# Reading the second layer's modulation rows in the two mixers instead of the first MLP's second product

## The chip, the cores and the metric

The kernel runs on one core of a Trainium2 chip, in one launch. The metric is device time in microseconds (us) of that launch, lower being better. The engines that matter here are TensorE (PE, matrix products, with its weight loads shown apart as PEld), VectorE (DVE), ScalarE (ACT), GpSimd (POOL, which here mostly issues transfers) and SyncE (SP, which issues most transfers, in order). Each engine works off its own list of instructions in order; semaphores tie the lists together.

## The reference, cut to what matters

The program is a trunk of two layers over a sequence of 1024 positions and width 1024. A conditioning vector c modulates every sub-layer:

```python
cond = jax.nn.silu(c)
for i in range(DEPTH):
    mod = cond @ ada_w[i] + ada_b[i]
    sh1, sc1, g1, sh2, sc2, g2 = jnp.split(mod[:, None, :], N_MOD, axis=-1)
    h = _modulate(_rmsnorm(x, norm_mix_g[i]), sh1, sc1)
    y = _s5_mixer(h, ...) if i % N_MIXERS == 0 else _ssd_mixer(h, ...)
    x = x + g1 * y
    h = _modulate(_rmsnorm(x, norm_mlp_g[i]), sh2, sc2)
    x = x + g2 * _sq_relu_mlp(h, mlp_w1[i], mlp_w2[i])
return _rmsnorm(x, final_norm_g)
```

The product `cond @ ada_w[i]` gives 6 x 1024 numbers for each layer. The kernel cuts each layer's into 48 rows: one row is a block of 128 output columns, whose 128 x 1024 weights (512 KB) are read and multiplied with the conditioning vector. Eight rows make one of the six vectors (shift, scale and gate of the mixer, then of the MLP). For the second layer the first two vectors (16 rows) are needed when the first MLP ends, since its output is normalised and modulated there for the second mixer; the third when the second mixer's output is added; the fourth to sixth in the second MLP.

## The kernel before, in words

Activations lie with the 1024 channels over eight blocks of 128 partitions and the sequence along the free dimension, in two halves of 512. Every matrix product is made of three passes: weights and activations are each split into a high part and a remainder, and `mm3` (lines 117 to 119) multiplies high by high, high by low and low by high. So each 512 KB weight tile is loaded by SP into one of four buffers of the pool `raw` (line 95), ScalarE writes its high part `whi` (line 84), VectorE its low part `wlo` (line 85), and only then is the load buffer free. The pair `whi`, `wlo` lies in a ring of further buffers, and is free again when TensorE has used it for both halves of the sequence.

The stages follow each other: the first mixer (S5) with its gated projection `glu` at 285 to 453 us, the first MLP's up product (`Up`) and second product (`mlp_down`) from 775 to 1098 us, the second mixer (`ssd_proj` and `ssd_group`) to about 1660 us, its output product, and the second MLP with the same two products (the second one from 2188 to 2498 us).

The gated projection runs over four passes (`mg` 0 to 3). A pass has two output blocks m, each with a value weight and a gate weight, so four weights of 512 KB, over both halves. The weights of the next pass are asked for at the end of a pass, and behind them the caller asks for modulation rows.

The second product of an MLP runs over seven sub-products of eight steps. A step loads and combines a weight tile, loads activations that were stored to memory, splits both on ScalarE and VectorE and makes 24 matmuls. The second mixer makes, for each of four groups of heads, six blocks of a convolution and four blocks of the gate z, each a weight tile over both halves; the chunks of the group before are worked off between these.

A modulation row is `mod_dot` (lines 329 to 334): SP loads the 512 KB, VectorE makes the dot product with an accumulator in one instruction (line 334), and after eight rows the bias is added (line 317). Where no pool of its own is named (`K.adap`), the row is loaded into the pool `raw`, so that it takes a turn among the weights' four load buffers; in the first MLP's second product it has two buffers of its own.

The code gives the order in which work is asked for. The order on each engine is set from it by a list scheduler when the program is built, and is fixed from then on.

## Time and profile before

| what | value |
|---|---|
| median of 3 runs | 2514.36 us (2514.31 to 2516.89) |
| span of the profiled execution | 2516.1 us |
| mean granted TensorE clock | 0.989 |
| TensorE, VectorE, ScalarE busy | 97%, 76%, 46% |
| DMA queue of SP and ScalarE, share of 16 engines | 47.8% |
| rows (line 334) | 88, 1220 ns each |

The profile is of one execution. Its times are us from the start of the span. Busy time by engine says how full an engine is; the chain of waits says which work ended last; the order of time and the busy time by stretches say what a single stage waits for. "PEclk" or "granted clock" is the share of full speed that TensorE was allowed. A row of the order of time has the start, the duration, the engine, the line, the operation and the tiles (written <- read), and in brackets how long the engine had been idle and what ended that. "SPq" rows are transfers being issued. The 88 dot products of line 334 are 40 of the first layer's 48 rows (the mixer's shift is made on TensorE) and the 48 of the second layer, of which the profile shows the latter from 796 to 1040 us.

### The profile page before, as it was taken

The page shows a single profiled execution, that of the slowest core. Times are in us where ns is not written, and L with a number is a line of the kernel's source. Part 1 is how long each engine was busy: PE and PEld are TensorE (multiplying, and loading weights), DVE is VectorE, ACT ScalarE, POOL GpSimd, SP SyncE. Part 2 cuts the span into 40 slices and gives each one's busy share as a digit, 9 for nine tenths or more (in the row PEclk, how much of TensorE's full clock was granted, in tenths as well). Part 3 has the DMA queues.
Part 4 walks back from the last instruction along what each step waited for, and adds up shares of the span by engine and source line. Part 5 has one row for each costly group of instructions (what it writes and reads, how often), then busy time and mean ns, then how long its engine had stood idle before and what let it go on. Part 6 is the DMA issues. An engine that isn't in the chain of part 4 may idle for free.

```text
span 2516.1 us, 32759 instructions
## 1 busy us (share of the span) xinstructions
PE 2445.6 (97%) x11624; PEld 1961.2 (78%) x11624; DVE 1913.1 (76%) x3265; ACT 1167.4 (46%) x1975; POOL 214.4 (9%) x400
## 2 busy tenths in 40 slices
PE   7999899999999999999999999999999999999997
PEld 3788788877777778877887878877888777788886
DVE  8798754978887898968585867789687777787664
ACT  4577412744444334534464645534246444444342
POOL 0010000122221000100000000000011222210000
PEclk8999999999999999999999999999999999999998
DMA  6576773467769999823554554574246666794752
GB/s 244 149 174 165 237 251 97 148 205 258 263 226 318 322 307 320 276 85 109 162 160 153 159 168 145 180 249 141 80 137 210 217 223 222 256 318 150 252 191 84
DMA packets 284643, 503.80 MB, mean 200 GB/s; under 512 B 22080, under 2 KB 162368, under 8 KB 284480
## 3 DMA queue, kind: packets, MB, share of 16 engines
q1 hardware_dynamic: 242496, 386.34, 47.8%
q0 software_dynamic: 32384, 106.98, 12.5%
q10 hardware_dynamic: 9600, 8.39, 1.0%
q8 instruction: 91, 1.49, 0.2%
q14 instruction: 72, 0.59, 0.1%
HBM read 364.27 MB, written 133.17 MB: 198 GB/s over the span
## 4 chain that ended last, share of the span: by engine, by line
PE 80%; DVE 7%; DMA 5%; ACT 3%; issue 2%; DVEq 0%; SPq 0%; ACTq 0%
PE pd L117 11%; PE pd L118 11%; PE pd L119 11%; PE py L117 4%; PE py L119 4%; PE py L118 4%; PE px L117 4%; PE px L119 3%; PE px L118 3%; PE pv L117 3%; PE pv L118 3%; PE pv L119 3%; PE pm L119 2%; PE pm L117 2%; PE pm L118 2%
## 5 line engine op out<-in xcount | busy, mean ns | idle before, releaser
L84 ACT CAST whi<-raw 128x1024 fp32r<-128x1024 f32 x241 | 251.0, 1047 | 360.5 <-PE pd L118 145.4
L85 DVE TENSOR_TENSOR wlo<-raw,whi 128x1024 fp32r<-128x1024 f32 x241 | 293.0, 1217 | 107.8 <-ACT whi L84 104.2
L334 DVE SCALAR_TENSOR_TENSOR ada<-ada,cond 128x1024 f32<-128x1024 f32 x88 | 107.0, 1220 | 57.6 <-DMA ada<-in_ada 57.3
L499 ACT ACTIVATE s<-s 128x512 f32<-128x512 f32 x84 | 53.0, 631 | 156.1 <-DVE s L497 153.6
L391 POOL DMA_DIRECT2D hscr<-x x32 | 17.4, 543 | 955.4 <-DVE x L758 752.5
L1257 DVE SCALAR_TENSOR_TENSOR cacc<-cr,conv,cacc 128x1024 f32<-128x1024 f32 x72 | 91.7, 1277 | 1.0 <-ACT cacc L1238 0.6
L1310 ACT ACTIVATE L<-csb,cs 128x128 f32<-128x128 f32 x224 | 69.9, 390 | 39.8 <-DMA csb<-csr 39.8
L506 POOL DMA_DIRECT2D b<-s x96 | 52.0, 542 | 319.9 <-ACT s L500 278.5
L497 DVE TENSOR_TENSOR s<-s,px 128x512 f32<-128x512 f32 x60 | 41.0, 683 | 34.4 <-PE px L119 34.4
L497 DVE TENSOR_TENSOR s<-s,pv 128x512 f32<-128x512 f32 x36 | 24.7, 686 | 55.1 <-PE pv L119 55.1
L506 POOL DMA_DIRECT2D b<-tt x96 | 52.0, 542 | 44.8 <-DVE tt L511 27.9
L500 ACT ACTIVATE s<-s 128x512 f32<-128x512 f32 x84 | 53.2, 633 | 2.7
L1261 ACT ACTIVATE cth<-cacc 128x512 f32<-128x512 f32 x48 | 27.7, 624 | 42.3 <-DVE cacc L1257 40.4
L673 DVE SCALAR_TENSOR_TENSOR x<-py,mod,x 128x512 f32<-128x512 f32 x40 | 27.6, 743 | 24.4 <-PE py L119 24.4
L209 ACT ACTIVATE sq<-x 128x512 f32<-128x512 f32 x28 | 16.7, 625 | 54.1 <-DVE x L673 49.1
L1330 DVE SCALAR_TENSOR_TENSOR y<-xs,cst,pm 128x128 f32<-128x128 f32 x128 | 38.2, 340 | 4.7 <-PE pm L1327 4.7
L117 PE MATMUL pd<-h00h,whi 128*128 128x512 f32 (+1 forms) x97 | 39.9, 413 | 1.8 <-ACT h00h L238 1.8
L1237 ACT COPY cr<-pd 128x512 f32<-128x512 f32 x48 | 27.8, 579 | 28.8 <-PE pd L119 28.8
L1128 ACT ACTIVATE gt<-pd,bgh 128x512 f32<-128x512 f32 x16 | 11.0, 685 | 63.9 <-PE pd L119 63.9
L117 PE MATMUL pd<-h01h,whi 128*128 128x512 f32 x97 | 39.5, 407 | 0.5 <-DVE h61h L758 0.5
L119 PE MATMUL pd<-h10h,wlo 128*128 128x512 f32 (+1 forms) x97 | 39.3, 405 | 0.0
L118 PE MATMUL pd<-h30l,whi 128*128 128x512 f32 (+1 forms) x97 | 38.9, 401 | 0.0
(1006 smaller groups left out, 8165.1 us busy)
## 6 DMA issues: line engine op xcount, KB each, us to landing
raw<-in_w SPq DMA_DIRECT2D x204, 512.0 KB, 4.7
br<-b SPq DMA_DIRECT2D x112, 512.0 KB, 5.4
ada<-in_ada SPq DMA_DIRECT2D x96, 512.0 KB, 5.3
b<-s POOLq DMA_DIRECT2D x96, 256.0 KB, 2.9
b<-tt POOLq DMA_DIRECT2D x96, 256.0 KB, 3.8
csb<-csr SPq DMA_DIRECT2D x32, 512.0 KB, 4.6
raw<-in_w_xbc SPq DMA_DIRECT2D x24, 512.0 KB, 4.3
xscr<-cacc SPq DMA_DIRECT2D x24, 512.0 KB, 2.7
```

The source lines that it names most:

```text
L84: K.nc.scalar.copy(hi, src)
L85: K.nc.vector.tensor_tensor(lo, src, hi.bitcast(F32), op=ALU.subtract)
L117: K.nc.tensor.matmul(ps, wh, xh, start=start and i == 0, stop=False, skip_group_check=more)
L118: K.nc.tensor.matmul(ps, wh, xl, start=False, stop=False, skip_group_check=more)
L119: K.nc.tensor.matmul(ps, wl, xh, start=False, stop=stop and i == n - 1, skip_group_check=more)
L334: K.nc.vector.scalar_tensor_tensor(r, r, 1.0, K.cond, op0=ALU.mult, op1=ALU.mult, accum_out=acc)
L497: nc.vector.tensor_tensor(t, t, p, op=ALU.add)
L499: nc.scalar.activation(t, t, AF.Relu)
L500: nc.scalar.activation(t, t, AF.Square)
L506: self.K.nc.gpsimd.dma_start(self.bscr[DOWN.index(nm)][m // 2][m % 2], t)
L1257: V.scalar_tensor_tensor(acc, cr[:, t:t + L], K.cw[:, i, t:t + 1], acc, op0=ALU.mult, op1=ALU.add)
L1310: nc.scalar.activation(Lm[:, r, :], cb[:, r, :], AF.Relu, bias=S.cs[:, c0 + r:c0 + r + 1], scale=-1.0)
```

## The change

The 48 rows of the second layer no longer belong to `mlp_down`; its parameter `extra` and the two calls of it are gone, as is the row pool's use there. The first 16 (shift and scale of the second mixer) are appended to the rows of the gated projection, which asks for up to 11 after each pass instead of up to 6: 11, 11 and 10 now, where it was 6, 6 and 4. The other 32 are asked for in the second mixer, one before each half of a z block (the condition `left < KT` holds for the eight yields of these halves in each group). In both places they use the pool `raw`. The conditioning vector's tile, 4 KB of each partition, stays allocated until the end of the second mixer.

```diff
-def mlp_down(K, pool, x, bscr, w2, gate, xscr, mid, extra):
+def mlp_down(K, pool, x, bscr, w2, gate, xscr, mid):
...
-        if q == 0:
-            extra()
-        if q not in (4, 5):
-            extra()
...
-        K.adap = K.br if cond else None
-        mlp_down(
-            K, K.br, x, K.bscr[i], io.w2[i], gate, K.hscr[i], lambda *a: mid(x, *a), lambda: next(mods, None)
-        )
-        drain(mods)
-        K.adap = None
+        mlp_down(K, K.br, x, K.bscr[i], io.w2[i], gate, K.hscr[i], lambda *a: mid(x, *a))
...
-    mod0 = mods(K, io.ada, 0, (3, 4))
+    def rows(*of):
+        for i, js in of:
+            yield from mods(K, io.ada, i, js)
+
+    mod0 = rows((0, (3, 4)), (1, (0, 1)))
...
     for _ in glu(K, x, io.x, g, io.s5_w_glu, us, begun, io.ada, mid):
-        for _ in range(6):
+        for _ in range(11):
             next(mod0, None)
...
-    mod1 = mods(K, io.ada, 1, (0, 1, 2, 3, 4, 5))
...
-    cond.release()
+    mod1 = mods(K, io.ada, 1, (2, 3, 4, 5))
...
-    pr = ssd_proj(K, cp, h, 0)
+
+    def project_in(g):
+        for left in ssd_proj(K, cp, h, g):
+            if left is not None and left < KT:
+                next(mod1, None)
+            yield left
+
+    pr = project_in(0)
...
-        pr = ssd_proj(K, cp, h_mix, gr)
+        pr = project_in(gr)
...
+    drain(mod1)
+    cond.release()
```

The order on the engines moves in three places. The first is SP's list of transfers in the gated projection, before the change. `raw<-in_s_w_glu` are the four weights of the fourth pass, `ada` are rows, `x` are tiles of the residual, and `raw<-in_w` the first weights of the MLP that follows.

```order
L333 DMA ada<-in_ada 128x1024
L268 DMA x_2791<-in_x 128x512
L268 DMA x_2792<-in_x 128x512
L268 DMA x_2789<-in_x 128x512
L268 DMA x_2790<-in_x 128x512
L333 DMA ada<-in_ada 128x1024 x6
L95 DMA raw<-in_s_w_glu 128x1024 x4
L333 DMA ada<-in_ada 128x1024 x6
L95 DMA raw<-in_w 128x1024 x21
```

The same piece with the change:

```order
L333 DMA ada<-in_ada 128x1024 x2
L268 DMA x_2791<-in_x 128x512
L268 DMA x_2792<-in_x 128x512
L333 DMA ada<-in_ada 128x1024 x3
L268 DMA x_2789<-in_x 128x512
L333 DMA ada<-in_ada 128x1024 x5
L268 DMA x_2790<-in_x 128x512
L333 DMA ada<-in_ada 128x1024 x2
L95 DMA raw<-in_s_w_glu 128x1024 x4
L333 DMA ada<-in_ada 128x1024 x12
L95 DMA raw<-in_w 128x1024 x21
```

Behind the fourth pass's weights stand twelve rows instead of six (ten rows and the two of the residual's gate that the fourth pass uses), and the batch before them is thirteen instead of eight.

The second place is VectorE's list in the same stage, at the end of the third pass. Before:

```order
L334 SCALAR_TENSOR_TENSOR ada,mac_3594<-ada,cond 128x1024
L1131 TENSOR_TENSOR x_2796<-x_2796,gv 128x512
L373 SCALAR_TENSOR_TENSOR mod<-mac_3594,cst 128x1
L374 TENSOR_SCALAR g1h<-mod 128x1
L1129 TENSOR_SCALAR gt<-gt,g1h 128x512
L1130 SCALAR_TENSOR_TENSOR gv<-pd,cst,gt 128x512
L1131 TENSOR_TENSOR x_2793<-x_2793,gv 128x512
L85 TENSOR_TENSOR wlo<-raw,whi 128x1024 x2
```

With the change (line numbers above 584 are four lower in the new kernel; `gt`, `gv` and `x` are the gating of a finished half):

```order
L1126 SCALAR_TENSOR_TENSOR gv<-pd,cst,gt 128x512
L334 SCALAR_TENSOR_TENSOR ada,macc<-ada,cond 128x1024
L1127 TENSOR_TENSOR x_2796<-x_2796,gv 128x512
L334 SCALAR_TENSOR_TENSOR ada,macc<-ada,cond 128x1024 x4
L1125 TENSOR_SCALAR gt<-gt,g1h 128x512
L1126 SCALAR_TENSOR_TENSOR gv<-pd,cst,gt 128x512
L334 SCALAR_TENSOR_TENSOR ada,macc<-ada,cond 128x1024
L1127 TENSOR_TENSOR x_2793<-x_2793,gv 128x512
L317 SCALAR_TENSOR_TENSOR mod<-macc,cst 128x8
L323 SCALAR_TENSOR_TENSOR G<-mod,cst 128x8
L334 SCALAR_TENSOR_TENSOR ada,mac_3639<-ada,cond 128x1024
L85 TENSOR_TENSOR wlo<-raw,whi 128x1024
```

The last row of each piece is the low part of the fourth pass's first weight (with the second weight's behind it before the change). Between the weight converted ahead of it and this one stood three rows; now nine do, seven of them in this piece.

The third place is VectorE's list in the second mixer, in one of the chunks of a group. `cr` and `cacc` belong to the convolution, `yz`, `L`, `ysq`, `ssq` and `st` to the chunk.

```order
L1278 TENSOR_TENSOR yz<-y,zl 128x512
L1308 TENSOR_SCALAR L<-csb,ncs 128x128
L1227 MEMSET cr 128x3
L334 SCALAR_TENSOR_TENSOR ada,macc<-ada,cond 128x1024
L1278 TENSOR_TENSOR ysq<-ysq 128x256
L1278 TENSOR_TENSOR ysq<-ysq 128x128
L1253 SCALAR_TENSOR_TENSOR cacc<-cr,conv,cacc 128x1024
L1348 COPY ssq<-pm 128x1
L1278 TENSOR_TENSOR st<-st,pm 128x512
```

The row stands among the chunk's own steps, where there was none; of a group's eight rows four stand so, one for each of four chunks, and the other four among the z blocks of the group before.

More of the change, by code (lines that the diff above doesn't have):

```diff
@@ L1467, in left, with mlp @@
         return tc.alloc_tile_pool(name=name, bufs=n, reuse_waits="tile")
-    def mlp(i, x, xa, up, pan, gate, mid, cond=None, mods=(), gates=()):
-        mods, gates = iter(mods), iter(gates)
+    def mlp(i, x, xa, up, pan, gate, mid, gates=()):
+        gates = iter(gates)
         K.wz = right("wz" + str(i), 2)
@@ L1642, in mid @@
         return norm_steps(K, x, f, each, bank, order)
-    mlp(0, x, xa, up, up.pan, modv(K, 0, 5), mid, True, mod1, gate0)
-    cond.release()
+    mlp(0, x, xa, up, up.pan, modv(K, 0, 5), mid, gate0)
+    mod1 = mods(K, io.ada, 1, (2, 3, 4, 5))
     K.wx = left("wx1", 2)
@@ L1678, in trunk @@
     x, x1 = h_new(), h_new()
-    h_mix = h
     up, mid = entry(1, x1, K.G[:, 24:32], modv(K, 1, 3))
```

## The prediction

> **What bounds the kernel now.** I read the page first, then the busy time by stretches, then the order of time around the places that the change touches.
>
> ```profile
> span 2516.1 us, 32759 instructions
> PE 2445.6 (97%) x11624; PEld 1961.2 (78%) x11624; DVE 1913.1 (76%) x3265; ACT 1167.4 (46%) x1975; POOL 214.4 (9%) x400
> PE 80%; DVE 7%; DMA 5%; ACT 3%; issue 2%; DVEq 0%; SPq 0%; ACTq 0%
> ```
>
> TensorE is busy 97% of the span and makes 80% of the chain of waits. So moving VectorE or DMA work is worth something only where TensorE stands still for it, or runs at a lower clock afterwards. The change leaves TensorE's own work alone. The question is which TensorE pauses go and which come.
>
> The kernel holds a control experiment: the second product of the MLP runs twice, in the first layer with the 48 rows and in the second without any. The columns are length, then busy time of PE, PEld, DVE, ACT, POOL, then granted clock, DMA share and GB/s.
>
> ```profile
> 775.00:1098.00 323.00, 315.51 (x1361) 256.81 (x1360) 272.92 (x427) 134.40 (x228) 19.05 (x35) 0.98 0.86 294
> 2188.00:2498.00 310.00, 309.99 (x1360) 254.19 (x1359) 211.23 (x311) 129.49 (x217) 10.92 (x20) 1.00 0.63 212
> ```
>
> The same work (1360 and 1359 weight loads recorded), 13.0 us apart. The difference sits in the second and third of the seven sub-products; the fourth, and the same two of the second layer, follow:
>
> ```profile
> 820.00:870.50 50.50, 47.25 (x195) 38.11 (x194) 43.57 (x76) 14.77 (x31) 3.28 (x6) 0.93 0.93 312
> 870.50:919.00 48.50, 45.74 (x193) 36.91 (x192) 47.93 (x81) 21.17 (x37) 0.00 (x0) 0.96 0.95 315
> 919.00:963.00 44.00, 44.00 (x193) 36.01 (x193) 43.09 (x66) 16.62 (x24) 0.00 (x0) 1.00 0.94 323
> 2232.20:2276.30 44.10, 44.10 (x194) 36.12 (x193) 40.98 (x68) 19.25 (x37) 2.74 (x5) 1.00 0.81 266
> 2276.30:2320.10 43.80, 43.80 (x194) 36.05 (x193) 29.04 (x43) 17.92 (x28) 0.00 (x0) 1.00 0.39 129
> ```
>
> 50.5 + 48.5 − 44.1 − 43.8 = 11.1 us. Of this 3.25 + 2.76 = 6.0 us are two pauses of TensorE, (1 − 0.93) × 50.5 + (1 − 0.96) × 48.5 = 5.5 us a lower clock. The pauses in the order of time, with the matmul before and two after the first:
>
> ```profile
> 849.21 0.39 PE L118 MATMUL pm<-h21l,whi 128*128 128x512 f32 x1
> 852.84 0.79 PE L119 MATMUL pm<-h21h,wlo 128*128 128x512 f32 x1 [3.25 <-DVE wlo L85]
> 853.86 0.63 PE L118 MATMUL pn<-h21l,whi 128*128 128x512 f32 x1
> 886.41 0.80 PE L119 MATMUL py<-h41h,wlo 128*128 128x512 f32 x1 [2.76 <-DVE wlo L85]
> ```
>
> Both end when VectorE delivers a weight's low part: the rows stand ahead of it on a VectorE that is 86% and 99% busy. The matmuls behind the pause take 0.63 instead of 0.39 us.
>
> **What is removed.** 48 rows (a 512 KB load and an L334 dot product) leave the stretch 775 to 1098. Its second copy says what is left: **−11.1 us** for the two sub-products. The other 1.9 us of the 13.0 lie at the stretch's entry and at its closing normalisation, which the rows need not cause. Bounds: −6 (one of the two pauses has another cause) to −13. I take −11.
>
> [...]
>
> **What is added in the gated projection.** 16 rows go to the stretch 285 to 453, where TensorE has hardly a pause so far and VectorE idles 41%:
>
> ```profile
> 285.00:453.40 168.40, 167.69 (x745) 137.90 (x744) 99.19 (x169) 42.99 (x56) 7.61 (x14) 1.00 0.55 181
> L334 DVE SCALAR_TENSOR_TENSOR ada<-ada,cond x22: 1214/1225/1227, 306.9 to 387.3; 128x1024 f32<-128x1024 f32 x22
>   DMA ada<-in_ada: 27.7, 15
> DMA to landing us min/median/max: 3.4/4.6/6.5
> ```
>
> VectorE time alone would be 16 × 1.3 = 21 us into 69 us of idle time: free. But the rows share four buffers and one in-order queue with the weights, and in that order nine of them now stand ahead of the first weight of the fourth pass, where three stood. I call its four weights, in the order in which VectorE converts them, w3, w4, w1, w2 (TensorE needs w1 first). Before:
>
> ```profile
> 362.08 1.22 DVE L85 TENSOR_TENSOR wlo<-raw,whi 128x1024 fp32r<-128x1024 f32 x1 [2.33 <-ACT whi L84]
> 366.84 1.23 DVE L334 SCALAR_TENSOR_TENSOR ada<-ada,cond 128x1024 f32<-128x1024 f32 x1 [1.62 <-DMA ada<-in_ada]
> 378.40 1.22 DVE L85 TENSOR_TENSOR wlo<-raw,whi 128x1024 fp32r<-128x1024 f32 x1 [0.76 <-ACT whi L84]
> 381.54 1.23 DVE L334 SCALAR_TENSOR_TENSOR ada<-ada,cond 128x1024 f32<-128x1024 f32 x1 [1.91 <-DMA ada<-in_ada]
> 384.40 1.23 DVE L334 SCALAR_TENSOR_TENSOR ada<-ada,cond 128x1024 f32<-128x1024 f32 x1 [1.22 <-DMA ada<-in_ada]
> 387.28 1.23 DVE L334 SCALAR_TENSOR_TENSOR ada<-ada,cond 128x1024 f32<-128x1024 f32 x1 [0.41 <-DMA ada<-in_ada]
> 400.17 1.23 DVE L85 TENSOR_TENSOR wlo<-raw,whi 128x1024 fp32r<-128x1024 f32 x1 [3.54 <-ACT whi L84]
> ...
> 352.79 7.32 SPq L95 DMA_DIRECT2D raw<-in_s_w_glu  x4
> 363.34 19.80 SPq L333 DMA_DIRECT2D ada<-in_ada  x6
> ...
> 404.95 0.39 PE L119 MATMUL pd<-h00h,wlo 128*128 128x512 f32 x1
> ```
>
> w1 is done at 401.4 and needed at 404.95: 3.6 us to spare. It cannot be done sooner, since its buffer is freed by the third pass at 400. Its raw copy and w2's hold two of the four load buffers, so the rows in between go through the other two, one every 2.9 us (381.54, 384.40, 387.28), and through one buffer while w4 waits too: 3.5 us from the issue at 363.34 to 366.84, plus 1.3.
>
> Step one, when the fourth pass's weights arrive. Ten more rows (five in each of the first two batches) go ahead of their loads. The present pace, and the idle time that can take some of it:
>
> ```profile
> 332.52 1.23 DVE L334 SCALAR_TENSOR_TENSOR ada<-ada,cond 128x1024 f32<-128x1024 f32 x1 [6.44 <-DMA ada<-in_ada]
> 338.20 1.23 DVE L334 SCALAR_TENSOR_TENSOR ada<-ada,cond 128x1024 f32<-128x1024 f32 x1 [2.46 <-DMA ada<-in_ada]
> 344.39 1.22 DVE L334 SCALAR_TENSOR_TENSOR ada<-ada,cond 128x1024 f32<-128x1024 f32 x1 [3.41 <-DMA ada<-in_ada]
> 355.01 1.23 DVE L334 SCALAR_TENSOR_TENSOR ada<-ada,cond 128x1024 f32<-128x1024 f32 x1
> ```
>
> Six rows start from 344.39 to 355.01, 2.1 us apart, so ten are 21 us, less 6.4 + 2.5 + 3.4 = 12.3 us of waiting that is filled at best: at least 9 us late. I take 12: w3 is converted at 374 instead of 362.
>
> Step two: first row 374 + 1.2 + 4.8 = 380, second 385, w4 at 386, then nine rows at 2.9 us with the first of them already on its way: 386 + 4 + 8 × 2.9 = 413. w1 follows, done at about 414.5. TensorE needs it at 405: a **pause of about 9 us**, and by the pairs above (6.0 us of pauses, 5.5 of clock) some 2 us at a lower clock behind it; the clock loss of one pause was 3.5 and 1.9 us. Together **+11 us**. Upper end 13 (9.5 + 3.5). Lower end: nothing late in step one gives w4 at 379.6 as now, 381 + 8 × 2.9 + 1.2 = 405.4, a pause of 0.5 us. The other weights have room: w2 is behind one more row and needed 5.4 us after w1.
>
> Behind the waiting rows on VectorE stand also the gating of the two halves finished at 395 and 406. Their PSUM banks are wanted again two halves later, over 20 us, so they cost nothing. The first MLP's weight loads, queued behind the twelve rows on SP, come some 25 us later than at 385.66 and are first used at 453.
>
> **What is added in the second mixer.** 32 rows, eight in each of four groups of heads. In each of the last three groups about four fall into the light stretch and four, one per chunk, into this one (first two rows; the third is the light one):
>
> ```profile
> 1260.00:1300.00 40.00, 39.93 (x211) 31.77 (x210) 35.10 (x63) 26.39 (x51) 0.00 (x0) 1.00 0.54 166
> 1300.00:1340.00 40.00, 40.00 (x230) 32.43 (x229) 36.21 (x66) 23.65 (x53) 0.00 (x0) 1.00 0.59 192
> 1340.00:1380.00 40.00, 39.22 (x191) 31.70 (x190) 18.05 (x41) 15.93 (x33) 0.00 (x0) 1.00 0.44 133
> ```
>
> 80 − 35.1 − 36.2 = 8.7 us of idle VectorE takes four rows of 1.3 us, and each row's load is issued a chunk (some 16 us) before VectorE comes to it, so landing (6.5 us at most above) is covered. The stretch 919 to 963 is the nearest row: VectorE 98% busy, eight rows in it, TensorE 44.00 of 44.00. Cover gone, all twelve such rows cost 16 us. But TensorE's order moves too. A group's last two chunks have 3 and 15 matmuls fewer to cover the way to their final reductions, 18 × 0.23 = 4.1 us (0.23 is 44.00 us over 193 in the stretch 919 to 963). VectorE is lighter there, since the convolutions are through. Bounds: −1 (the 0.8 us pause in the third row goes) to 3 × 4.1 = 12; I take **+2**, three times the 0.7 us of the last chunk, which has a pause already.
>
> **Sum.** −11 + 11 + 2 = +2 us. The profiled execution's span, 2516.1, would become 2518.1; it is one execution, and the median of the three runs is 2514.36, 1.7 less. On that basis: **2516 us**.
>
> **Rivals.**
>
> *The projection holds (faster).* If the loads of the fourth pass arrive in time, its pause is 0.5 us: −11 + 0.5 + 1 = −9.5, 2505 us (1 for a calmer mixer). For it: VectorE idles 41% there and no TensorE pause names it now. Against it: w1 has only 3.6 us to spare behind nine rows on two buffers, and even six us less delay leaves a pause of 3 us.
>
> *VectorE becomes the bound in the chunks (slower).* Place: 1260 to 1340 and the two stretches like it. A row may cost 8.7 / 4 = 2.2 us before the chunk chain falls behind TensorE; it does if a row waits over 0.9 us for its load. The fifteen rows in the projection that waited did so for 27.7 / 15 = 1.85 us; then 1.3 + 1.85 − 2.2 = 0.95 us × 12 = 11 us, and the total is −11 + 11 + 11, 2525 us. The matmuls that cover less (12 us) would end at the same time. For it: 90% busy, in order. Against: the chunk of lead, and the 98% stretch without a pause.
>
> *The first MLP gains little.* If only the 6.0 us of pauses return and the lower clock has another cause, the total is −6 + 11 + 2 = +7, 2521 us; the same if late loads make the pauses (DMA 0.93 busy and more there) and half stays. Against both: the second layer's copy, at clock 1.00 with DMA 0.81 and 0.39. [...] That the rows are not moved at all is excluded by the order of instructions.
>
> **Chances and range.** Forecast 0.48, with its own range of 2511 to 2521; the projection holds 0.26; chunks bound 0.18; little gained 0.08. A difference under 0.2% (5 us) cannot be told from none here. Faster is the first rival and hardly any of the forecast: 0.27. Slower is the other two and a part of the forecast above 2519.4: 0.31. Same: 0.42. The range takes in the first and most of the second rival: 2504 to 2526.
>
> **What would show it.** In the first MLP's second product the two pauses gone, clock 1.00, its length near 311 us. In the gated projection one TensorE pause at about 405 that a weight's low part ends, of 4 to 12 us, with clock below 1.00 behind it. In the mixer no pause over 1.5 us. The forecast is wrong if the projection keeps its length, if the first MLP keeps its pauses, or if the mixer's pauses add up to more than 6 us.

## The result, and the profile after

| | before | with the change |
|---|---|---|
| median | 2514.65 us (2514.31 to 2516.89, 4 runs) | 2539.24 us (2532.74 to 2541.56, 4 runs) |
| ratio | 1 | 1.0094, 95% interval 1.008 to 1.0109 |
| span of the profiled execution | 2516.1 us | 2539.8 us |
| mean granted TensorE clock | 0.989 | 0.987 |

The change makes the kernel 24.6 us slower. The forecast was 2516 us with a range of 2504 to 2526, so it was wrong. One execution among those reported below, 6159 us with the other quotas in the gated projection where the other three took 2524 to 2526 us, is left out of its ratio. The head of the profile's page with the change:

```profile
span 2539.8 us, 32827 instructions
PE 2454.3 (97%) x11624; PEld 1964.6 (77%) x11624; DVE 1914.1 (75%) x3265; ACT 1169.9 (46%) x1975; POOL 214.5 (8%) x400
```

TensorE has the same 11624 matmuls and VectorE the same 3265 instructions in 1914.1 us (1913.1 before). Nothing was added to the work. TensorE's busy time rose by 8.7 us, for the most part matmuls at a lower clock (it was busy for 48.3 us at half clock, 35.8 before), and its idle time by 15.0 us (2539.8 − 2454.3 against 2516.1 − 2445.6). To see where, the matmuls of both traces are counted in order and the same one is compared at each boundary between stages. How much longer each stage became (profiled executions, us):

| stage, by the times of before | change |
|---|---|
| up to 301 (ahead of the rows that moved) | −1.1 |
| gated projection, 301 to 480 | +11.6 |
| first MLP's up product, 480 to 787 | +2.9 |
| first MLP's second product, 787 to 1099 | −12.1 |
| second mixer and its output product, 1099 to 1875 | +24.1 |
| second MLP's up product, 1875 to 2196 | −0.9 |
| the rest | −0.8 |

**The first MLP's second product** gave back what was expected. By stretches, the whole and then two that together hold the second and third sub-products (833.6 to 921.5 us), which had the two pauses (length, busy PE, PEld, DVE, ACT, POOL, granted clock, DMA share, GB/s):

```profile
788.50:1099.00 310.50, 309.81 (x1360) 254.04 (x1359) 219.68 (x322) 137.63 (x228) 19.05 (x35) 1.00 0.66 225
...
833.50:880.00 46.50, 46.50 (x205) 38.09 (x204) 43.49 (x72) 20.91 (x40) 2.74 (x5) 1.00 0.74 251
880.00:922.00 42.00, 42.00 (x186) 34.56 (x185) 26.89 (x40) 16.78 (x26) 0.00 (x0) 1.00 0.41 138
```

310.5 us instead of 323.0, TensorE busy all the time in both stretches, clock 1.00.

**The gated projection** shows the predicted pause. VectorE's list in order of time, the fourth pass's weights being the three L85 rows (w3, w4, w1), with the rows between the first and the last of the nine left out; then TensorE's first matmul that needs w1, and SP's issue of the twelve rows:

```profile
374.39 1.23 DVE L85 TENSOR_TENSOR wlo<-raw,whi 128x1024 fp32r<-128x1024 f32 x1 [1.81 <-ACT whi L84]
379.40 1.23 DVE L334 SCALAR_TENSOR_TENSOR ada<-ada,cond 128x1024 f32<-128x1024 f32 x1 [3.78 <-DMA ada<-in_ada]
384.19 1.23 DVE L334 SCALAR_TENSOR_TENSOR ada<-ada,cond 128x1024 f32<-128x1024 f32 x1 [1.56 <-DMA ada<-in_ada]
385.57 1.22 DVE L85 TENSOR_TENSOR wlo<-raw,whi 128x1024 fp32r<-128x1024 f32 x1
388.99 1.23 DVE L334 SCALAR_TENSOR_TENSOR ada<-ada,cond 128x1024 f32<-128x1024 f32 x1 [2.19 <-DMA ada<-in_ada]
...
410.72 1.23 DVE L334 SCALAR_TENSOR_TENSOR ada<-ada,cond 128x1024 f32<-128x1024 f32 x1 [0.50 <-DMA ada<-in_ada]
411.87 1.22 DVE L85 TENSOR_TENSOR wlo<-raw,whi 128x1024 fp32r<-128x1024 f32 x1
```

```profile
413.14 0.80 PE L119 MATMUL pd<-h00h,wlo 128*128 128x512 f32 x1 [9.15 <-DVE wlo L85]
...
375.65 34.04 SPq L333 DMA_DIRECT2D ada<-in_ada  x12
```

Nine rows from 388.99 to 410.72 are 2.7 us apart, w1 is done at 413.1 and TensorE has waited 9.15 us.

**The second mixer** is where the 24 us came from. The sums over the stretch from the same first to the same last matmul (1098 to 1675 us before, 1099 to 1700 us now), before and after:

```profile
sum 577.00, PE 573.11 PEld 458.74 DVE 430.82 ACT 300.00 POOL 1.14; mean PE 143.28 PEld 114.69 DVE 107.70 ACT 75.00 POOL 0.28
```

```profile
sum 601.00, PE 583.37 PEld 463.70 DVE 466.30 ACT 298.49 POOL 1.14; mean PE 145.84 PEld 115.92 DVE 116.57 ACT 74.62 POOL 0.28
```

601 − 577 = 24 us, of which TensorE's idle time rose from 3.9 to 17.6 us (13.7) and its busy time by 10.3 us, most of it lower clock behind the pauses (TensorE was busy for 15.4 us in four stretches at 0.50; before the change the clock was 1.00). VectorE took 35.5 us more, about what 32 rows of 1.2 us come to, but it still idles 135 of 601 us: it is not full. Its idle time in front of the rows there, and the time from a row's issue to its landing:

```profile
  DMA ada<-in_ada: 30.9, 11
...
DMA to landing us min/median/max: 3.4/4.2/7.7
```

VectorE stood still 30.9 us, in front of 11 of the 32 rows. The worst place is the first chunk of each group. `ysq` is the sum of squares that VectorE makes in two steps and TensorE finishes at line 1347. VectorE, then TensorE, then SP's issues in the order of time:

```profile
1232.96 0.43 DVE L1278 TENSOR_TENSOR ysq<-ysq 128x256 f32<-128x256 f32 x1 [0.70 <-ACT ysq L1343]
1236.87 1.23 DVE L334 SCALAR_TENSOR_TENSOR ada<-ada,cond 128x1024 f32<-128x1024 f32 x1 [3.48 <-DMA ada<-in_ada]
1238.02 0.08 DVE L334 DVE_READ_ACCUMULATOR ada<-ada,cond 128x1 f32 x1
1238.02 0.29 DVE L1278 TENSOR_TENSOR ysq<-ysq 128x128 f32<-128x128 f32 x1
```

```profile
1238.45 0.56 PE L1347 MATMUL pm<-ones,ysq 128*128 128x1 f32 x2 [3.50 <-DVE ysq L1278]
...
1386.83 0.35 PE L1347 MATMUL pm<-ones,ysq 128*128 128x1 f32 x2 [4.34 <-DVE ysq L1278]
...
1537.57 0.56 PE L1347 MATMUL pm<-ones,ysq 128*128 128x1 f32 x2 [3.80 <-DVE ysq L1278]
```

```profile
1228.61 1.22 DVE L85 TENSOR_TENSOR wlo<-raw,whi 128x1024 fp32r<-128x1024 f32 x1
...
1228.12 0.92 SPq L1338 DMA_DIRECT2D zl<-zscr  x2
1229.10 0.49 SPq L95 DMA_DIRECT2D raw<-in_w_z  x1
1229.86 0.35 SPq L333 DMA_DIRECT2D ada<-in_ada  x1
```

A row stands between the two steps of the reduction. It waits 3.48 us for its own load, TensorE's matmul behind it 3.50 us. The load went out at 1229.86 us, when a weight's conversion (1228.61 + 1.22) had given its buffer back, right behind a weight's and two `zl` loads, and its data were there at 1236.84 us. That is 7.0 us from issue to landing; the rows in front of the other two pauses took 7.7 and 7.3 us, and these three are the slowest of the 32 (median 4.2). So two things make such a row late: when its load goes out, and how long it takes there.

### The profile page after: what moved, and what is told of

Same layout as the page of the kernel before. It is cut to its first block, busy times and chain, and to the rows that moved or that the text cites. A ratio compares the mean times of both kernels' runs of the same rounds, so it can differ in the third digit from the quotient of the medians.

```text
span 2539.8 us, 32827 instructions
## 1 busy us (share of the span) xinstructions
PE 2454.3 (97%) x11624; PEld 1964.6 (77%) x11624; DVE 1914.1 (75%) x3265; ACT 1169.9 (46%) x1975; POOL 214.5 (8%) x400
## 4 chain that ended last, share of the span: by engine, by line
issue 63%; PE 22%; POOL 6%; DVE 3%; DMA 3%; ACT 1%; POOLq 0%; DVEq 0%; SPq 0%; ACTq 0%
POOL b L506 3%; PE py L117 2%; PE py L119 2%; PE py L118 2%; PE pm L117 1%; PE pm L118 1%; PE pm L119 1%; PE pd L118 1%; PE pd L117 1%; PE pd L119 1%; PE pm L1081 1%; PE px L117 1%; PE px L119 1%; PE px L118 1%; POOL hscr L391 1%
## 5 line engine op out<-in xcount | busy, mean ns | idle before, releaser
L85 DVE TENSOR_TENSOR wlo<-raw,whi 128x1024 fp32r<-128x1024 f32 x241 | 293.4, 1218 | 99.7 <-ACT whi L84 94.3
L119 PE MATMUL pd<-h00h,wlo 128*128 128x512 f32 (+1 forms) x97 | 38.9, 401 | 9.2 <-DVE wlo L85 9.2
L628 DVE TENSOR_TENSOR raw<-raw 128x1024 f32<-128x1024 f32 x16 | 19.6, 1225 | 30.8 <-DMA raw<-in_w 27.5
L118 PE MATMUL pd<-h11l,whi 128*128 128x512 f32 x97 | 39.4, 406 | 0.0
L1323 PEld LDWEIGHTS pm<-L,xdt 128*64 128x64 f32 x512 | 27.3, 136 | 15.5 <-DVE L L1278 8.4
```

The lines of the kernel that those rows point to most:

```text
L85: K.nc.vector.tensor_tensor(lo, src, hi.bitcast(F32), op=ALU.subtract)
L118: K.nc.tensor.matmul(ps, wh, xl, start=False, stop=False, skip_group_check=more)
L119: K.nc.tensor.matmul(ps, wl, xh, start=False, stop=stop and i == n - 1, skip_group_check=more)
```

## The experiments

Fifteen kernels were run, each against the kernel before on the same chip. In the diffs "-" is the changed kernel, and "..." stands for lines left out. "Stage" times are changes against the kernel before by the same matmul, as in the table above, from one profiled execution each. Where a stage is the same as with the change, they say how far to trust them: the projection shows +10.4 to +12.9 us in seven such runs, the mixer +19.2 to +26.1 in three.

### Where the rows stand in the mixer, and whether they are loaded

The first run moves the rows in the mixer, the second takes their loads away.

```diff
-            if left is not None and left < KT:
+            if left is not None and 5 <= left <= 12:
```

> The changed kernel, but in the second mixer the eight rows of a group are asked for earlier: before the last five halves of the convolution blocks and the first three halves of the z blocks, so that no row stands between the two halves of the first chunk's reduction. The work is the same. Late loads (a row that waits for its own load holds up the reduction behind it): the three pauses of 3.5 to 4.3 us at 1238, 1387 and 1538 us go, with the half clock behind them; 16 to 22 us of the mixer's 24 us come back, about 2520 us. VectorE's work (32 dot products too many for the mixer, wherever they stand): within 3 us of 2539. TensorE's own order (fewer matmuls to cover the last chunks): within 5 us of 2539.

Measured: 2529.44 us (ratio 1.0067, 1.0045 to 1.0089), 15.1 us over the kernel before on its chip, where the change was 24.6 us over. In the profiled execution (span 2525.5 us) the mixer and its output product cost +6.6 us instead of +24.1. The three pauses of the first chunks are gone; what stays in the chunks are two elsewhere, of the same kind:

```profile
1343.65 1.23 DVE L334 SCALAR_TENSOR_TENSOR ada<-ada,cond 128x1024 f32<-128x1024 f32 x1 [1.52 <-DMA ada<-in_ada]
1344.80 0.08 DVE L334 DVE_READ_ACCUMULATOR ada<-ada,cond 128x1 f32 x1
1344.80 0.75 DVE L1278 TENSOR_TENSOR ysq<-ysq 128x256 f32<-128x256 f32 x2
```

```profile
1345.69 0.35 PE L1347 MATMUL pm<-ones,ysq 128*128 128x1 f32 x2 [1.60 <-DVE ysq L1278]
...
1488.37 0.35 PE L1347 MATMUL pm<-ones,ysq 128*128 128x1 f32 x2 [2.79 <-DVE ysq L1278]
```

The same 32 dot products at other places cost a quarter in the mixer: VectorE's work as such is not the price. The total came 9 us above the 2520 expected; its four runs lie 13.6 us apart (2522.34 to 2535.91), so the sum is less sure than the stage.

```diff
-    K.nc.sync.dma_start(r, w)
-    K.nc.vector.scalar_tensor_tensor(r, r, 1.0, K.cond, ..., accum_out=acc)
+    if not K.noload:
+        K.nc.sync.dma_start(r, w)
+    K.nc.vector.scalar_tensor_tensor(
+        r, K.cond if K.noload else r, 0.0 if K.noload else 1.0, K.cond, ..., accum_out=acc)
```

> The changed kernel, but the 32 rows of the second mixer are not loaded: the dot product runs on the conditioning vector, times zero, with the same size and the same buffer, so the second layer's gate of the mixer and its MLP's shift, scale and gate are left out of the computation (only their biases remain). Late loads: the mixer is within 4 us of its time before the change, about 2519 us in all, although a row still stands between the halves of a reduction. VectorE's work: the mixer stays above +18 us, over 2533 us. TensorE's own order: the pauses stay, over 2530 us.

Measured: 2518.56 us (ratio 1.0018, 1.0008 to 1.0028); mixer +3.2 us. One row now stands ahead of the same reduction and one between its two steps, and they hold it up only by their own length:

```profile
1229.81 1.22 DVE L335 SCALAR_TENSOR_TENSOR ada<-cond 128x1024 f32<-128x1024 f32 x1
...
1230.96 0.42 DVE L1279 TENSOR_TENSOR ysq<-ysq 128x256 f32<-128x256 f32 x1
1231.29 1.22 DVE L335 SCALAR_TENSOR_TENSOR ada<-cond 128x1024 f32<-128x1024 f32 x1
1232.44 0.08 DVE L335 DVE_READ_ACCUMULATOR ada<-cond 128x1 f32 x1
1232.44 0.28 DVE L1279 TENSOR_TENSOR ysq<-ysq 128x128 f32<-128x128 f32 x1
```

So the loads make about 21 of the 24 us; 32 dot products without them cost 3. Both runs also moved some of TensorE's and VectorE's instructions in the mixer, so the order was not held fixed; that it is the loads is also read directly from the rows above, where TensorE's pauses of 3.50, 4.34 and 3.80 us follow VectorE's waits of 3.48, 4.22 and 3.84 us for a row's data.

### The gated projection

Loads taken away from the rows asked for after its passes (same edit as above), and the same rows with other quotas:

> The changed kernel, but the rows of the gated projection that are asked for after its passes are not loaded: their dot products run on the conditioning vector, times zero (the first MLP's shift and scale and the second mixer's shift and scale are left out of the computation). Late loads behind four shared buffers: no pause of 9 us at 404 to 413 us, that stage is within 2 us of its time before the change, 2526 to 2529 us in all. VectorE's own work ahead of the fourth pass's weight: a pause of at least 5 us stays there, over 2533 us.

```diff
+    q = [16, 14, 2, 0]
...
-        for _ in range(11):
+        for _ in range(q.pop(0)):
             next(mod0, None)
```

> The changed kernel with the same 40 rows in the gated projection, but 16, 14 and 2 of them asked for after its first three passes instead of 11, 11 and 10, so that four rows instead of nine stand on VectorE ahead of the fourth pass's first weight. If these nine make the pause, it is under 1 us there and 2525 to 2529 us in all. If the sum of loads through four buffers makes it, a pause of over 5 us stays there or moves to the pass before, 2533 us or more.

Measured: 2524.61 us (1.0034 to 1.0064), a little under what was expected, and 2525.07 us (1.0028 to 1.0059); in both the pause is gone and the stage's cost is 0.0 us instead of +11.6. With the other quotas all 40 rows are still loaded, and the fourth pass's first weight is converted when its buffer is free:

```profile
397.16 1.22 DVE L334 SCALAR_TENSOR_TENSOR ada<-ada,cond 128x1024 f32<-128x1024 f32 x1
400.67 1.22 DVE L85 TENSOR_TENSOR wlo<-raw,whi 128x1024 fp32r<-128x1024 f32 x1
```

Four rows stand ahead of it now. So it is the nine rows ahead of that weight, with their loads, and neither their number in the stage nor the bytes.

### Each part undone alone

Rows of the undone part go to the first MLP's second product, with two buffers of their own as before, but asked for later and one at a time: for the projection's 16 rows steps of `q in (2, 3)`, as in the diff, for the mixer's 32 rows `q in (2, 3, 5, 6)`.

```diff
+        if q in (2, 3):
+            extra()
...
-    mod0 = rows((0, (3, 4)), (1, (0, 1)))
+    mod0 = rows((0, (3, 4)))
...
-        for _ in range(11):
+        for _ in range(6):
```

> The changed kernel with only the gated projection's part undone: its quotas are 6 again, and the 16 rows of the second mixer's shift and scale are read in the first MLP's second product, one per step of the third and fourth sub-products, from two buffers of their own. The 32 rows stay in the second mixer. If the parts add up (+11.6 us there), 2524 to 2529 us. If the rows cost again where they go, 2532 us or more.

> The changed kernel with only the mixer's part undone: the 32 rows are read in the first MLP's second product, one per step of the third, fourth, sixth and seventh sub-products and four behind them, from two buffers of their own. The 16 rows stay in the gated projection. If the parts add up (+24 us in the mixer), 2514 to 2519 us. If the 32 rows bring back a pause in that product, 2521 to 2526 us.

Measured: 2526.11 us (1.0037 to 1.0065) with the projection undone, 2518.67 us (1.0011 to 1.0034) with the mixer undone. The parts add up. By stages: projection 0.0 and mixer +25.4 in the first, projection +11.0 and mixer −1.3 in the second. The second product kept −12.1 and −10.8 us, with 16 and 32 rows in it. VectorE does not take these rows in the sub-product where they are asked for, but mostly earlier: in the first to fifth sub-product 1, 7, 8, 0 and 0 of them start with the projection undone, and 1, 7, 12, 8 and 4 with the mixer undone. Before the change it was 7, 15, 9, 9 and 2, and six in the sixth. So rows are free in the second and third sub-products too, seven in one and twelve in the other, and the two pauses of before go with 22 rows in the first two. The one pause left over 1 us (1.02 us, mixer undone) is in the fifth.

### Spreading the rows

Three versions take the rows to other places, to test that a row is free wherever nothing waits behind it, and to find a kernel faster than both. The first has eight rows in the first MLP's up product (behind the eight of its own gate, which move from its fifth step to its first), 32 at `q in (2, 3, 4, 5)` of the second product and eight in the second MLP's up product.

> None of the 48 rows in the gated projection or the second mixer: eight in the first MLP's up product, 32 in its second product but only one per step of sub-products two to five (third to sixth) with two buffers of their own, and eight in the second MLP's up product. If the loss in the second product before the change came from the rows' density in its first sub-products (two, then one per step, where VectorE and the transfers are fullest), the 11 us come back and nothing is paid elsewhere: 2502 to 2507 us. If any row in that product costs, 2510 to 2516 us.

Measured: 2515.00 us (0.9993 to 1.0012), no gain. That lies in the second range that was expected, but only a part of the price is in the second product (−8.3 us instead of −12.1, a pause in the fifth sub-product); the larger part, +10.9 us, is in the first MLP's up product.

```profile
537.81 0.50 PE L117 MATMUL px<-h01h,whi 128*128 128x512 f32 x1 [3.31 <-DVE s L490]
...
981.64 0.50 PE L118 MATMUL py<-h61l,whi 128*128 128x512 f32 x1 [1.85 <-DVE h61l L85]
```

Eight rows more, with the gate's eight moved forward, cost nearly as much in the up product as 48 did where they had been.

> The 48 rows once more without the places that paid: none in the gated projection, none in the first MLP's up product, none in the fifth sub-product of its second product. 24 rows in that product (one per step of the third, fourth and sixth sub-products, own buffers), eight at the first group's convolution in the second mixer, before any chunk runs, eight in the second mixer's output product, eight in the second MLP's up product. If rows cost only where VectorE is full or where they wait for a shared buffer in front of a reduction or weight, all of these are free, and the 11 us of the first MLP's second product stay: 2503 to 2507 us. If any row costs about 0.25 us wherever it stands (the 11 us over 48), 2512 to 2517 us.

Measured: 2508.07 us (0.9965 to 0.9984): 6 us faster than before the change, a little outside the expected range. Two stages showed a price. In the fifth sub-product TensorE pauses for 2.33 us at 973.18. The rows are not what stands there, as was expected of the next run: the last of this product's 24 starts on VectorE at 931.28 us, in the fourth. VectorE waits for a weight's load instead, and why that load is late is not shown:

```profile
968.66 1.23 DVE L628 TENSOR_TENSOR raw<-raw 128x1024 f32<-128x1024 f32 x1 [3.77 <-DMA raw<-in_w]
```

And the second MLP's up product cost +3.1 us; with the same eight rows at the same place it showed −0.6 in the run before, so no price of the place is shown.

```diff
+        if q in (2, 3, 6):
+            extra()
+        if q == 6:
+            extra()
...
+            if left is not None and 5 <= left <= 12:   # first group of heads only: eight rows
...
-    drain(outs)
+    for at in outs:                    # the second mixer's output product: 16 rows
+        next(mod2, None)
+        if at[0] == 2:
+            next(mod2, None)
```

> The spread of 48 rows without the two places that still showed a cost: no row in the sixth sub-product of the first MLP's second product (its rows were pulled ahead into the fifth, where a pause of 2.3 us stood) and none in the second MLP's up product (some 3 us there). Instead: 16 rows in the third and fourth sub-products, one per step, eight in the seventh, two per step; eight at the first group's convolution; 16 in the second mixer's output product. If the remaining costs were of these places, 2502 to 2506 us. If rows cost as much in the output product, 2507 to 2511 us as the spread before.

Measured: 2505.23 us (2502.97 to 2511.44, 12 runs), ratio 0.9972 (0.9961 to 0.9982): 7.3 us faster than the kernel before, the best of all, and within what was expected. Its stages: projection 0.0, second product −12.1, mixer and output +0.1.

```profile
span 2501.8 us, 32801 instructions
PE 2437.7 (97%) x11624; PEld 1957.2 (78%) x11624; DVE 1912.1 (76%) x3265; ACT 1170.8 (47%) x1975; POOL 213.7 (9%) x400
```

Its second, third and fourth sub-products, in which 8, 12 and 3 rows start (the rows asked for in the seventh are taken as early as these):

```profile
819.00:863.00 44.00, 44.00 (x193) 36.06 (x192) 43.48 (x73) 19.17 (x38) 2.73 (x5) 1.00 0.97 341
863.00:907.00 44.00, 44.00 (x195) 36.20 (x194) 39.00 (x66) 18.10 (x29) 0.00 (x0) 1.00 0.71 240
907.00:951.00 44.00, 44.00 (x194) 36.03 (x193) 35.90 (x49) 16.77 (x24) 0.00 (x0) 1.00 0.83 279
```

### Why the mixer's rows get their data late

Four ways to get a row's data sooner: a fifth shared buffer (with its control), an earlier request, another queue, and buffers of their own.

```diff
-    K.raw = perm("raw", bufs=4)
+    K.raw = perm("raw", bufs=5)
...
-    return K.tmp.tile([P, 512], F32, tag="t", bufs=6, name=name)
+    return K.tmp.tile([P, 512], F32, tag="t", bufs=4, name=name)
```

> The changed kernel with five load buffers instead of four in the pool that rows and weights share; to make room, the pool of temporaries of 512 columns has four buffers instead of six. If a free load buffer is what late loads wait for, the pause in the gated projection shrinks from 9 us to under 4 (rows go through three buffers, some 2.0 us apart instead of 2.7) and the mixer's loss from 24 us to under 14: 2516 to 2528 us. If loads are late because they are asked for late, or because they land slowly, 2533 us or more.

> The control for the one before: the changed kernel with only the temporaries' pool cut from six to four buffers, four load buffers as they were. If these temporaries matter nowhere, within 3 us of 2539; if they do, slower, and the run with five load buffers is read against this one.

Measured: 2625.54 us with five buffers and 2637.88 us for the control, so the expected totals were off by 100 us for a reason outside the question: four temporaries cost +46.0 and +52.1 us in the two up products. By stages against the control, the fifth buffer takes the projection from +12.0 to +0.3 us, the mixer only from +21.4 to +20.9. In the projection a free buffer is what the rows wait for, as far as a run can show it in which the order on the engines moved too; in the mixer a fifth one makes no difference that could be told from the spread:

```profile
1277.25 0.52 PE L1347 MATMUL pm<-ones,ysq 128*128 128x1 f32 x2 [4.99 <-DVE ysq L1278]
```

```diff
+        coming = load(n + 1) if n + 1 < 8 * len(js) else None   # the next row's load
...
+        K.nc.vector.scalar_tensor_tensor(                        # this row's dot product
...
-    mod1 = mods(K, io.ada, 1, (2, 3, 4, 5))
+    mod1 = mods_ahead(K, io.ada, 1, (2, 3, 4, 5))
```

> The changed kernel, but in the second mixer a row's load is asked for one half of a z block (some 5.5 us) before its dot product, through the same four buffers. If rows wait because their loads are asked for too late, the pauses of 3.5 to 4.3 us in front of the reductions go, 2520 to 2528 us. If a load starts when a shared buffer comes free, however early it is asked for, the pauses stay: 2533 to 2543 us.

Measured: 2542.46 us (1.01 to 1.0134); mixer +22.4; the first-chunk pauses are 4.53, 4.03 and 3.08 us. Asking earlier gains nothing.

```diff
-    K.nc.sync.dma_start(r, w)
+    (K.nc.gpsimd if K.apart else K.nc.sync).dma_start(r, w)   # apart: in the second mixer
```

> The changed kernel with the same order on VectorE, but in the second mixer the rows' loads are issued by GpSimd instead of SP, so that they no longer stand in SP's queue behind the loads of z, which wait until z's store has landed in memory. With four load buffers the row in front of the reduction also needs a buffer that a weight's conversion gives back at 1229.8 us, at the same time as SP came to it (1229.9). If the buffer alone still holds it, the pauses stay: 2533 us or more. If the place behind z in SP's queue is what counts, they shrink to under 1.5 us each: 2518 to 2528 us.

> The kernel with five load buffers and four temporaries, its order on VectorE unchanged, with the rows' loads of the second mixer issued by GpSimd. Neither a buffer nor SP's queue holds the load now. If these two hold it together, the mixer's three long pauses (5.0, 2.1 and 5.6 us with five buffers alone) go and the total falls by 12 to 22 us from 2625 to 2603 to 2613. If loads are late because the transfers themselves are slow there (7 us to land), the pauses stay and the total is above 2619.

Measured: 2550.01 us (1.0131 to 1.0175) and 2629.61 us (ratio 1.0458, 1.043 to 1.0486). The expected gain of the second did not come: mixer +30.8 and +28.4, worse than with SP. The first-chunk pauses stay (4.77, 4.30 and 4.68 us with four buffers, 2.87, 4.17 and 3.90 us with five), and with four a new one of 5.34 us stands in the mixer's set-up. SP's queue alone is not what holds the load. The second outcome is the one that had been expected if the transfers themselves are slow there, and the rows in front of these pauses did take 6.1 to 8.1 us to land, against medians of 4.7 and 4.5. But the issue still hangs on the buffers: by GpSimd, too, the 32 loads go out 0.2 to 0.9 us after VectorE frees one, with four buffers and with five.

What the traces share: the weights in the pool are loaded far ahead of their use. Pairing loads and conversions in order, the changed kernel has all four buffers taken for 472 of the 493 us from 1150 on; a weight issued at 1195.19 is converted at 1248.62. At 1229.9 three buffers hold weights, and the rows pass through the one that is left: the row's load is issued as soon as VectorE frees a buffer (the conversion quoted above ends at 1228.61 + 1.22 = 1229.83, the load goes out at 1229.86), takes 3.4 to 7.7 us to land, and only then comes the dot product that frees it again. Of the 32 rows' loads with the change, 21 go out within 0.04 us of the end of a conversion or dot product, the other eleven within 1.6. By the same pairing the kernel with five buffers has all five taken for 473 of 488 us: the fifth fills as well. That leaves buffers of their own:

```diff
-                next(mod1, None)
+                K.adap = cp                 # two buffers of the mixer's own pool
+                next(mod1, None)
+                K.adap = None
...
-        yz = T("yz", [P, 4, P], 2)
+        yz = T("yz", [P, 4, P], 1)
```

> The changed kernel with two load buffers of their own for the rows of the second mixer. To make room, the temporaries have four buffers instead of six, as in the control with four (2638 us), and the chunk's product with z has one instead of two. The order on VectorE then has all 32 rows in the first group's projection, ahead of the first chunk's reduction. If the rows waited because weights loaded far ahead hold three of the four shared buffers, so that rows pass through the last one singly, the mixer's loss of about 21 us against the kernel before the change falls under 6: 2617 to 2624 us in all. If the transfers or VectorE's work make the loss, over 2630 us.

Measured: 2639.77 us, against 2637.88 for its control. The total does not confirm it, the trace does in part. All 32 rows are now worked off between 1161 and 1295 us, and in the chunks nothing over 2.4 us is left of the control's pauses (4.89, 2.89, 1.51 and 3.57 us at line 1347). But the rows, no longer held back, stand on VectorE ahead of the mixer's set-up, and TensorE waits there instead:

```profile
1247.85 1.19 PE L1203 MATMUL pd<-adt,tri 128*128 128x256 f32 x2 [12.56 <-DVE adt L1145]
```

The mixer costs +17.5 us against +21.4, a difference within the spread. Since the rows left the chunks, this run does not isolate the shared pool. What the runs show is that the rows' loads are the price (3.2 us are left without them), that the place decides (+6.6 us at other places), and that neither one more shared buffer nor an earlier request nor another queue helps. That weights loaded far ahead leave the rows a single buffer is read from the order of loads and conversions. How much of each long wait is the late issue and how much the slow landing stays open: had the row at 1236.87 landed in the median 4.2 us, it would have waited some 0.7 us instead of 3.48 (an estimate, 3.48 less 7.0 − 4.2). Rows held at their places, with buffers of their own, were not tried and would settle it.

## Why the prediction was wrong

**What is removed: right.** −11 us for the two sub-products by their copy in the second layer; measured −12.1, in the trace of the change and in every kernel without rows there. The two sub-products alone gave 98.9 − 87.9 = 11.0 us. Of the 1.9 us that had been set aside as the stretch's edges, 0.9 belonged to the closing sub-product with six rows (the sixth, 43.0 to 42.1 us). TensorE's clock was 1.00, so the lost clock was of the pauses, and the rival in which little is gained fell.

**The gated projection: right, step by step, one step by choice.** Forecast: w3 at 374, rows at 380 and 385, w4 at 386, nine rows 2.9 us apart, w1 done at 414.5, a pause of 9 us, +11 us. Measured: 374.39, 379.40, 384.19, 385.57, 2.7 us apart, 413.1, 9.15 us, +11.6. The 12 us by which w3 comes later were picked above a worked-out bound of 9; measured 12.3, so that the pause came out so near is in part luck. The rival in which the projection holds fell.

**The second mixer: wrong, +2 for +24.1.** This is the step that failed: the rows that fall into VectorE's light stretch were given no price. "Each row's load is issued a chunk (some 16 us) before VectorE comes to it" came out for the full stretches, for which it was worked out: in each of the last three groups the last three rows start 13.8 to 16.7 us after their issue, and none of them waits. For the light stretch nothing was worked out, and there the lead does not exist: the load goes out only when a buffer comes free, and the rows that waited there started 4.0 to 7.8 us after it, all of it landing. VectorE is half idle there (11.2 of 20 us busy from 1220 on, 10.5 of 20 from 1380 on), and just there the rows cost most: a row in front of a reduction step holds an idle VectorE until its data come, and TensorE with it, 3.50, 4.34 and 3.80 us. The stretch 919 to 963, which served as evidence that rows are free (it held nine, not eight), has rows on buffers of their own. The upper bound of 12 us counted lost cover, and no bound contained a row's wait for its load in the light stretch. The price was in the prediction's own numbers: it had used "one row every 2.9 us" through two buffers in the projection and did not ask how many buffers the weights leave in the mixer.

**The slower rival: half of the mechanism.** It had a row waiting for its load, but at VectorE's full stretches, decided by how full VectorE is, at 11 us and 18%. The dot products without loads (+3.2 us) show that fullness plays hardly a part. A chance of 18% was too low for a wait that the projection's trace already showed fifteen times.

**The sum.** −12.1 + 11.6 + 24.1 = +23.6; the other stages add 0.1, and the spans differ by 23.7 us (the medians by 24.6). The first MLP's up product, which the prediction does not mention, shows +2.9 in the profiled execution: lower clock behind two pauses of 1.79 and 1.36 us (0.51 over the next 3.5 us, 0.50 over the next 3.4), while before the change it stayed at 1.00 behind the same two (1.31 and 1.37 us). In other runs with that stage unchanged it is −0.7 to +4.0, so it is no fixed price of the change.

On the clock: behind the pause of 9.15 us it is down for nearly all of the next 4.9 us (0.52), and is then whole (1.00). That is 4.9 × (1 − 0.52) = 2.4 us, where some 2 us had been forecast.

```profile
413.10:418.00 4.90, 4.86 (x12) 3.85 (x13) 3.94 (x9) 0.00 (x0) 0.00 (x0) 0.52 0.90 307
418.00:440.00 22.00, 22.00 (x99) 18.20 (x98) 5.93 (x9) 4.77 (x8) 1.08 (x2) 1.00 0.22 80
```

A shorter pause was followed by a lower clock too: behind the one of 1.36 us it was 0.50 for 3.4 us (last section).

## What to carry to other kernels

Ask of a load not when the program asks for it but when its buffer comes free, and who else draws on the pool: where operands fetched far ahead hold the others, a late guest passes through the last one, load after load, as the order of loads reads here. An instruction that waits for data is harmless on a busy or an idle engine alike only if nothing that another engine waits for stands behind it in order; "the engine is half idle there" does not make a place free (VectorE was busy for 11.2 and 10.5 of 20 us where TensorE paused for 3.50 and 4.34 us). When work has to be spread, measure the price of each place by stages against the same matmul, and look in the trace where the scheduler has put it: prices here ran from 0 to three quarters of a microsecond for the same row (24.1 us for 32 of them).

## What the runs showed that had not been expected

- Two of the six temporaries of 512 columns are worth 98 us: with four, the two up products take 46.0 and 52.1 us longer than before the change, TensorE waiting for the sums of line 490 and for weights' high parts (line 84). The two groups of the first up product that wait longest (busy and mean of one, then idle time before them and what ended it):

```profile
L117 PE MATMUL px<-h01h,whi 128*128 128x512 f32 x16 | 7.9, 494 | 18.0 <-DVE s L490 17.4 <-ACT s L488 0.7
...
L117 PE MATMUL px<-t20h,whi 128*128 128x512 f32 x16 | 7.5, 469 | 10.9 <-ACT whi L84 9.3 <-ACT s L488 1.6
```

- Issued by GpSimd, the rows' loads in the mixer took no less time to land (median 4.7 us, 4.2 by SP), and the mixer became slower (+30.8 us, against +19.2 to +26.1 with the same order by SP).
- A short pause was followed by a lower clock in one trace and not in the other. In the traces before and with the change all changes of the clock lie whole multiples of 3.41 us apart, and the stretches at half clock from 62 to 2500 us, five before and ten with the change, took 3.41, 6.83 or 10.24 us. The pause of 1.36 us that ends at 665.68 us and smaller ones leave TensorE idle for 1.58 of the 3.40 us up to such a change, and the next 3.40 us run at 0.50; in the same place before the change the pause of 1.37 us is all the idle time of the 3.40 us, and the next run at 1.00. The rows, with the change and before:

```profile
663.60:667.00 3.40, 1.82 (x8) 0.85 (x6) 3.29 (x5) 2.92 (x4) 1.63 (x3) 1.00 0.55 216
667.00:670.40 3.40, 3.40 (x10) 2.55 (x9) 3.08 (x5) 0.00 (x0) 0.54 (x1) 0.50 0.89 294
```

```profile
650.50:653.90 3.40, 2.03 (x9) 1.20 (x7) 3.29 (x6) 2.91 (x4) 1.11 (x3) 1.00 0.68 274
653.90:657.30 3.40, 3.19 (x14) 2.30 (x14) 3.40 (x5) 0.35 (x1) 1.08 (x2) 1.00 0.92 286
```

  With both traces cut into stretches of 3.41 us at those instants (62 to 2490 us), half clock followed none of 1381 stretches at full clock with under 1.5 us of idle TensorE, five of eight with 1.5 to 2.0 us, and all ten with more.
